# Expert down product in 512-column halves of two k-tiles, and the overflow branch at the second expert

## The chip, the cores and the metric

One core of a Trainium2 chip runs the kernel. The metric is the device time of one execution in microseconds (us); shown is the median of three runs. Engines: PE is TensorE (matmul), with PEld for its weight loads, DVE is VectorE, ACT is ScalarE, POOL is GpSimd, and SP is SyncE, whose queue issues the weight transfers from memory.

## What is computed

Two decoder layers on 256 tokens of 1024 features, all in float32. Layer 0 is a gated short convolution and a dense SwiGLU; layer 1 is dilated sliding-window attention and a mixture of experts. A final norm follows. The change touches the mixture alone:

```python
def moe_swiglu(h, w_router, w_gate, w_up, w_down):
    logits = jnp.einsum('bsd,de->bse', h, w_router)
    top_val, top_idx = lax.top_k(logits, TOP_K)            # 2 of 8
    top_w = jax.nn.softmax(top_val, axis=-1)
    gates = jnp.sum(jax.nn.one_hot(top_idx, N_EXPERTS) * top_w[..., None], axis=-2)
    for e in range(N_EXPERTS):
        out = out + gates[..., e:e + 1] * swiglu(h, w_gate[e], w_up[e], w_down[e])
```

`w_gate[e]` and `w_up[e]` are 1024 x 2816 and `w_down[e]` is 2816 x 1024, so each expert brings 34.6 MB of weights. The result is multiplied by the layer's gate row G (1024 values, the same for all tokens) and added to the residual x.

## The kernel before

The tokens of an expert are counted and placed in slots. A pair of experts gets its tokens gathered (`gather`, a product with a 0/1 matrix) as columns of `xg`, up to 128 per expert, in groups of 32. The first two groups are always computed. Groups 2 and 3 stand inside `by_groups`: a branch of PE on the count (over 64 at L1415, over 96 at L1417), which jumps over their instructions. More than 128 tokens of one expert go to `overflow()`, a long straight-line path behind a branch of PE, ACT, DVE and POOL at L1502, which stands ahead of expert 6 (`e == NE - 2`).

Per expert there are three rounds of gate and up products (1024, 1024 and 768 columns), each of two blocks of four loads, and then the down product in four blocks of 3, 3, 3 and 2 loads (`DOWN`). A load is two k-tiles, 1 MB in most. A block (`block`) takes its loads from the stream, multiplies them for groups 0 and 1, turns half of the activations of the round before (`turned`, `activated`), then branches to the other groups, then gives the loads back. `st.add_slot` lists the buffers for loads: at the end there are 17. SyncE issues the loads in the order of their use, each as soon as its slot is free.

A product keeps 32 token columns as weights and streams the expert's weight matrix through PE, four products side by side on four strips of 32 columns, so that a PSUM bank's 128 rows hold four results of 32 tokens. A float32 product shows in the trace as two LDWEIGHTS and two MATMUL. In gate/up (`use`, L1512 to L1517) the strips are gate and up times two halves of the columns, 512 columns each. In the down product (`use`, L1540 to L1544) they are four pieces of 256 of the 1024 output columns, and all k-tiles add up in the same rows. Four multiplications at L1554 weigh the four groups' banks with G4 (G in the same four pieces) into `og`.

PSUM: `groups()` gives four banks. Two are one of two `mm` tiles that are rotated each round (`sums_of`); the other two, for groups 2 and 3, are always the tile `rest`. The way back (`back`) runs after the first block of the next expert's first round: it multiplies `og` with a 0/1 matrix `GT` (`spread`) that puts each slot to its token, 32 rows at a time in four strips side by side, one piece of 256 columns each, into four banks (two halves of the other `mm` tile, two `tp` tiles), and eight DVE operations at L1493 add it to x with the token's weight.

The last expert runs its down product in three pieces of columns (`LAST`), with strips for k-tiles instead of columns, and has its own way back (`last_back`, L1561).

The order of instructions on each engine is that of the program; waits between engines come from the tiles that are written and read.

Of the kernel before, what the change touches and what calls it, by code (L numbers as in the profile page):

```python
# [10 lines left out]
F32 = mybir.dt.float32  # L11
# [7 lines left out]
P = 128  # L19
D = 1024  # L20
S = 256
# [31 lines left out]
def trunk_kernel(ctx: ExitStack, tc: tile.TileContext, a, out):  # L53
# [633 lines left out]
    slotc = cst.tile([P, 4], F32, name="slotc")  # L687
    slot = None

    def make_routing():  # L690
        nonlocal slot

        part = cst.tile([P, 4], I32, name="part")
        gp.iota(part, pattern=[[0, 4]], base=0, channel_multiplier=1)
        ve.tensor_scalar(part, part, 31, None, op0=OP.bitwise_and)
        partf = cst.tile([P, 4], F32, name="partf")
        ve.tensor_copy(partf, part)
        gp.iota(slotc, pattern=[[32, 4]], base=1, channel_multiplier=0, allow_small_or_imprecise_dtypes=True)
# [544 lines left out]
    def spread(e):  # L1243
# [5 lines left out]
        for g in range(4):  # L1249
            ve.tensor_scalar(GT[:, g], p[:, :S], slotc[:, g:g + 1], None, op0=OP.is_equal)  # L1250
# [110 lines left out]
    for n in range(2 * N_SPLIT):  # L1361
# [14 lines left out]
    st.add_slot("acc_g", lambda: [pers.tile([P, 1024], F32, name="rawa", tag="acc_g"),  # L1376
                                  moe.tile([P, 1024], F32, name="rawg")])
# [26 lines left out]
    G4 = moe.tile([P, 256], F32, name="G4")  # L1404
    for c in range(4):
        r = slice(32 * c, 32 * c + 32)
        sc.activation(G4[r], mods[3].G[r, 256 * c:256 * c + 256], AF.Copy)
# [67 lines left out]

    def back(e, n):

        ps = [sums_of[1][:, :512], sums_of[1][:, 512:], turn_tile(), turn_tile()]
        GT = GTs[e]

        def part(g):
            for i in range(NT):
                for c in range(4):
                    r = slice(32 * c, 32 * c + 32)
                    mm(ps[c][:, 256 * i:256 * i + 256], GT[r, g, i * P:(i + 1) * P], og[r, g], g == 0 and i == 0,
                       g == 3 and i == NT - 1)
        for g in range(2):
            part(g)
        by_groups(n, part)
        for i in range(NT):  # L1490
            for c in range(4):
                cs = slice(256 * c, 256 * c + 256)
                ve.scalar_tensor_tensor(x[:, i, cs], ps[c][:, 256 * i:256 * i + 256], gates[:, i, e:e + 1], x[:, i, cs],  # L1493
                                        op0=OP.mult, op1=OP.add)

    for e in range(NE):
        pr, b = divmod(e, 2)
        n_before, n_of = n_of, nc.values_load(counts[0:1, e:e + 1], engines=[mybir.EngineType.PE], min_val=0, max_val=S)
        if e == NE - 2:
# [53 lines left out]
        for g in range(4):  # L1553
            ve.tensor_mul(og[:, g], bank[g][:, :256], G4)  # L1554
# [90 lines left out]
```

## Time and profile before

| | |
|---|---|
| runs, median of three (lowest, highest) | 1230.16 us (1227.57, 1233.21) |
| the profiled execution, and its span | 1232.34 us, 1230.2 us |
| PE busy, PEld busy | 1103.3 us (90%), 671.8 us (55%) |
| DVE busy, ACT busy, POOL busy | 528.4 us (43%), 308.0 us (25%), 31.7 us (3%) |
[...]
| read from memory | 395.45 MB, 322 GB/s over the span |

An engine's busy time counts its instructions, not whether they ran at the engine's pace. Idle time before an instruction is put down to what ended last of what it waited for; "issue" is time in which it waited for nothing that the profile shows, and PEq is PE's own sequencer, as in a branch. A DMA share of 1 means that the core's 16 DMA engines were busy all the time (it can show a little more). Rows that the prediction uses stand in a section of their own below.

### The profile page before, as it was taken

The page shows a single profiled execution, that of the slowest core. Times are in us where ns is not written, and L with a number is a line of the kernel's source. Part 1 is how long each engine was busy: PE and PEld are TensorE (multiplying, and loading weights), DVE is VectorE, ACT ScalarE, POOL GpSimd, SP SyncE. Part 2 cuts the span into 40 slices and gives each one's busy share as a digit, 9 for nine tenths or more (in the row PEclk, how much of TensorE's full clock was granted, in tenths as well). Part 3 has the DMA queues.
Part 4 walks back from the last instruction along what each step waited for, and adds up shares of the span by engine and source line. Part 5 has one row for each costly group of instructions (what it writes and reads, how often), then busy time and mean ns, then how long its engine had stood idle before and what let it go on. Part 6 is the DMA issues. An engine that isn't in the chain of part 4 may idle for free. (4 is left out here: it accounts for less than half of the span.)

```text
span 1230.2 us, 23934 instructions
## 1 busy us (share of the span) xinstructions
PE 1103.3 (90%) x10346; PEld 671.8 (55%) x10346; DVE 528.4 (43%) x859; ACT 308.0 (25%) x497; POOL 31.7 (3%) x54
## 2 busy tenths in 40 slices
PE   3999979999999999987988998999999997697896
PEld 0799679998878876333343243435334434234333
DVE  1599768888779867320311210220211130130224
ACT  2344425444444473310110110110010020010021
POOL 3010100000001000000000000000000000000000
PEclk9899989999999999999989999999999998799999
DMA  6989767787837915999999999799689999799993
GB/s 248 331 313 342 241 244 269 278 320 291 307 113 279 338 55 196 406 407 407 404 408 405 404 408 395 274 395 399 225 344 405 361 388 407 288 365 407 405 373 125
DMA packets 139555, 398.82 MB, mean 324 GB/s; under 512 B 11427, under 2 KB 22459, under 8 KB 139402
## 3 DMA queue, kind: packets, MB, share of 16 engines
q1 hardware_dynamic: 138826, 396.47, 84.8%
q8 instruction: 125, 2.05, 0.7%
q14 instruction: 28, 0.23, 0.0%
q0 software_dynamic: 576, 0.07, 0.0%
HBM read 395.45 MB, written 1.05 MB: 322 GB/s over the span
## 5 line engine op out<-in xcount | busy, mean ns | idle before, releaser
L73 PE MATMUL mm<-raw,xg 128*32 128x512 f32 (+1 forms) x1624 | 234.7, 557 | 24.3 <-PEq L1502 8.1
L220 DVE TENSOR_TENSOR wlo<-raw,whi 128x1024 fp32r<-128x1024 f32 (+2 forms) x130 | 154.0, 1221 | 31.8 <-ACT whi L218 31.1
L218 ACT ACTIVATE whi<-raw 128x1024 fp32r<-128x1024 f32 (+2 forms) x130 | 132.2, 1045 | 126.3 <-PE mm L73 90.4
L1423 ACT ACTIVATE gu<-mm 64x512 f32<-64x512 f32 (+1 forms) x96 | 51.5, 551 | 447.5 <-PE mm L73 397.0
L73 PE MATMUL mm<-hTl,whi 128*128 128x256 f32 x544 | 148.6, 287 | 7.6 <-DVE hTl L531 7.6
L73 PE MATMUL mm<-rawr,xg 128*32 128x512 f32 (+1 forms) x1176 | 149.2, 570 | 5.8 <-PEq L1415 3.0
L73 PE MATMUL mm<-hTh,whi 128*128 128x256 f32 x544 | 151.3, 293 | 1.4 <-ACT hTh L530 1.4
L73 PE MATMUL mm<-hTh,wlo 128*128 128x256 f32 x544 | 147.9, 285 | 0.8 <-DVE wlo L220 0.8
L73 PEld LDWEIGHTS mm<-raw,xg 128*32 128x32 f32 x1624 | 70.5, 110 | 130.0 <-issue 120.8
L1424 DVE TENSOR_TENSOR gu<-gu,mm 64x512 f32<-64x512 f32 (+1 forms) x96 | 62.0, 646 | 182.0 <-ACT gu L1423 181.5
L73 PEld LDWEIGHTS mm<-hTl,whi 128*128 128x128 f32 x544 | 102.5, 194 | 10.9 <-DVE hTl L531 7.8
L73 PEld LDWEIGHTS mm<-hTh,whi 128*128 128x128 f32 x544 | 103.8, 198 | 3.9 <-ACT hTh L530 2.1
L73 PEld LDWEIGHTS mm<-hTh,wlo 128*128 128x128 f32 x544 | 102.4, 194 | 1.0 <-DVE wlo L220 1.0
L73 PE MATMUL mm<-rawr,acts 128*32 128x256 f32 x1280 | 80.3, 394 | 11.7 <-PEq L1415 3.9
L73 PE MATMUL mm<-raw,acts 128*32 128x256 f32 (+1 forms) x1168 | 79.0, 401 | 12.9 <-issue 5.6
L73 PEld LDWEIGHTS mm<-rawr,xg 128*32 128x32 f32 x1176 | 45.2, 110 | 79.1 <-issue 75.5
L1554 DVE TENSOR_TENSOR og<-mm,G 128x256 f32<-128x256 f32 x28 | 10.3, 418 | 178.2 <-PE mm L73 173.5
L73 PEld LDWEIGHTS mm<-rawr,acts 128*32 128x32 f32 x1280 | 42.9, 112 | 46.1 <-issue 18.7
L73 PEld LDWEIGHTS mm<-raw,acts 128*32 128x32 f32 x1168 | 41.2, 113 | 46.3 <-issue 25.1
L1435 DVE COPY acts<-tp 128x256 f32<-128x256 f32 (+1 forms) x48 | 19.3, 402 | 95.1 <-ACT acts L1241 94.7
L73 PE MATMUL mm<-rawx,xg 128*32 128x512 f32 (+1 forms) x272 | 56.0, 547 | 0.6 <-PEq L1417 0.5
L1493 DVE SCALAR_TENSOR_TENSOR x<-mm,gates,x 128x256 f32<-128x256 f32 x28 | 12.2, 477 | 97.6 <-PEq L1415 58.6
(271 smaller groups left out, 1462.6 us busy)
## 6 DMA issues: line engine op xcount, KB each, us to landing
rawr<-in_moe_w_down_dram SPq DMA_DIRECT2D x66, 512.0 KB, 10.1
raw<-in_mod_w_dram SPq DMA_DIRECT2D x64, 512.0 KB, 5.3
raw<-in_moe_w_down_dram SPq DMA_DIRECT2D x31, 1024.0 KB, 13.4
raw<-in_moe_w_gate_dram SPq DMA_DIRECT2D x26, 1024.0 KB, 12.2
raw<-in_moe_w_up_dram SPq DMA_DIRECT2D x25, 1024.0 KB, 12.8
rawr<-in_moe_w_up_dram SPq DMA_DIRECT2D x48, 512.0 KB, 11.5
rawr<-in_moe_w_gate_dram SPq DMA_DIRECT2D x48, 512.0 KB, 11.5
raw<-in_mod_w_dram SPq DMA_DIRECT2D x16, 1024.0 KB, 6.0
```

What stands on the lines that cost most here:

```text
L73: pe.matmul(o, l, r, start=start, stop=stop, skip_group_check=True)
L218: sc.activation(hi[:n, :c1 - c0], src, AF.Copy)
L220: ve.tensor_sub(lo_, src, f32(hi)))
L1423: sc.activation(a[64:, :N], bank[g][:64, :N], AF.Silu)
L1424: ve.tensor_mul(a[64 * g:64 * g + 64, :N], a[64:, :N], bank[g][64:, :N])
L1435: copy(acts[:, 8 * r:8 * r + 2 * nb, g:g + 32].rearrange("p (j m) t -> p m j t", j=2), v[:, :, n])
L1493: ve.scalar_tensor_tensor(x[:, i, cs], ps[c][:, 256 * i:256 * i + 256], gates[:, i, e:e + 1], x[:, i, cs], op0=OP.mult, op1=OP.add)
L1554: ve.tensor_mul(og[:, g], bank[g][:, :256], G4)
```

## The change

The down product takes two pieces of 512 columns instead of four of 256. The four strips are now two pieces times two k-tiles: strips 0 and 1 hold the sums of the even and the odd k-tile of each load for columns 0 to 511, strips 2 and 3 the same for 512 to 1023. `weighed` adds the halves: ACT copies the strip of one k-tile beside the other (32 x 512), DVE adds the two, and DVE multiplies with G2. Groups 0 and 1 are put one above the other, so that piece 0 of `og` has 64 rows per half of the columns; groups 2 and 3 are pieces 1 and 2 with 32 rows. The way back follows: piece 0 is one product of 64 rows and 512 columns for each tile of tokens and half, and DVE adds four results of 512 columns to x. The slot numbers that `spread` compares with get seven columns instead of four: three for this arrangement, four for the last expert's.

The place of G2 is that of `acc_g`, and the weight slot `acc_g` (with its other half `rawg`) is no longer given to the stream. The overflow branch stands ahead of expert 1 instead of expert 6.

```diff
--- before.py
+++ after.py
@@ -684,18 +684,21 @@
     upper = cst.tile([P, P], BF16, name="upper")
     ones_b = cst.tile([P, P], BF16, name="ones_b")
     ident_b = cst.tile([P, P], BF16, name="ident_b")
-    slotc = cst.tile([P, 4], F32, name="slotc")
+    slotc = cst.tile([P, 7], F32, name="slotc")
     slot = None
 
     def make_routing():
         nonlocal slot
 
-        part = cst.tile([P, 4], I32, name="part")
-        gp.iota(part, pattern=[[0, 4]], base=0, channel_multiplier=1)
-        ve.tensor_scalar(part, part, 31, None, op0=OP.bitwise_and)
-        partf = cst.tile([P, 4], F32, name="partf")
+
+        part = cst.tile([P, 7], I32, name="part")
+        gp.iota(part, pattern=[[0, 7]], base=0, channel_multiplier=1)
+        partf = cst.tile([P, 7], F32, name="partf")
+        for c, n, m, base, step in ((0, 2, 63, 1, 64), (2, 1, 63, 97, 0), (3, 4, 31, 1, 32)):
+            c = slice(c, c + n)
+            ve.tensor_scalar(part[:, c], part[:, c], m, None, op0=OP.bitwise_and)
+            gp.iota(slotc[:, c], pattern=[[step, n]], base=base, channel_multiplier=0, allow_small_or_imprecise_dtypes=True)
         ve.tensor_copy(partf, part)
-        gp.iota(slotc, pattern=[[32, 4]], base=1, channel_multiplier=0, allow_small_or_imprecise_dtypes=True)
         ve.tensor_add(slotc, slotc, partf)
         nc.sync.dma_start(rw, a["router_w"][0].rearrange("(k p) e -> p k e", p=P))
         gp.iota(tri, pattern=[[1, NE], [-1, NE]], base=0, channel_multiplier=0, allow_small_or_imprecise_dtypes=True)
@@ -1246,8 +1249,8 @@
         for i in range(NT):
             mm(p[:, i * P:(i + 1) * P], pxb[:, i], ident_b, i == 0, i == NT - 1)
         GT = moe.tile([P, 4, S], F32, name="GT")
-        for g in range(4):
-            ve.tensor_scalar(GT[:, g], p[:, :S], slotc[:, g:g + 1], None, op0=OP.is_equal)
+        for n, g in enumerate(range(3, 7) if e == NE - 1 else range(3)):
+            ve.tensor_scalar(GT[:, n], p[:, :S], slotc[:, g:g + 1], None, op0=OP.is_equal)
         GTs[e] = GT
 
     def overflow():
@@ -1373,8 +1376,6 @@
     remainder_h(1, 0)
     shifted(1, 1)
     st.add_slot("rows", lambda: pers.tile([P, 2048], F32, name="raw", tag="rows"))
-    st.add_slot("acc_g", lambda: [pers.tile([P, 1024], F32, name="rawa", tag="acc_g"),
-                                  moe.tile([P, 1024], F32, name="rawg")])
     st.topup()
     round_h(1, 1)
     most = moe.tile([P, 1], F32, name="most")
@@ -1401,10 +1402,10 @@
     ve.tensor_scalar(over, most, P + 0.5, None, op0=OP.is_gt)
     for t in turn_of:
         ve.memset(t, 0.0)
-    G4 = moe.tile([P, 256], F32, name="G4")
-    for c in range(4):
-        r = slice(32 * c, 32 * c + 32)
-        sc.activation(G4[r], mods[3].G[r, 256 * c:256 * c + 256], AF.Copy)
+    G2 = pers.tile([P, 512], F32, name="G2", tag="acc_g")
+    for h in range(2):
+        r = slice(64 * h, 64 * h + 64)
+        sc.activation(G2[r], mods[3].G[r, 512 * h:512 * h + 512], AF.Copy)
 
     fg = acts = og = n_of = pxb = None
     trans = None
@@ -1473,30 +1474,41 @@
         bk = [sums_of[0], rest]
         return [bk[g // 2][:, g % 2 * 512:g % 2 * 512 + 512] for g in range(4)]
 
+    def weighed(bank):
+
+
+        for g in range(4):
+            p, n = ((0, 0), (0, 1), (1, 0), (2, 0))[g]
+            for c in range(2):
+                r, q = (slice(k, k + 32) for k in (64 * c + 32 * n, 64 * c + 32 - 32 * n))
+                half = pers.tile([P, 512], F32, name="half", tag="rtmp", bufs=3)
+                sc.activation(half[r], bank[g][q], AF.Copy)
+                ve.tensor_add(og[r, p], bank[g][r], half[r])
+                if g != 0:
+                    r = slice(64 * c, 64 * c + (64 if g == 1 else 32))
+                    ve.tensor_mul(og[r, p], og[r, p], G2[r])
+
     def back(e, n):
 
-        ps = [sums_of[1][:, :512], sums_of[1][:, 512:], turn_tile(), turn_tile()]
+        ps = [[sums_of[1][:, :512], sums_of[1][:, 512:]], [turn_tile(), turn_tile()]]
         GT = GTs[e]
 
-        def part(g):
+        def part(p):
             for i in range(NT):
-                for c in range(4):
-                    r = slice(32 * c, 32 * c + 32)
-                    mm(ps[c][:, 256 * i:256 * i + 256], GT[r, g, i * P:(i + 1) * P], og[r, g], g == 0 and i == 0,
-                       g == 3 and i == NT - 1)
-        for g in range(2):
-            part(g)
-        by_groups(n, part)
+                for c in range(2):
+                    q = slice(64 * c, 64 * c + (32 if p else 64))
+                    mm(ps[i][c], GT[q, p, i * P:(i + 1) * P], og[q, p], p == 0, p == 2)
+        part(0)
+        by_groups(n, lambda g: part(g - 1))
         for i in range(NT):
-            for c in range(4):
-                cs = slice(256 * c, 256 * c + 256)
-                ve.scalar_tensor_tensor(x[:, i, cs], ps[c][:, 256 * i:256 * i + 256], gates[:, i, e:e + 1], x[:, i, cs],
-                                        op0=OP.mult, op1=OP.add)
+            for c in range(2):
+                cs = slice(512 * c, 512 * c + 512)
+                ve.scalar_tensor_tensor(x[:, i, cs], ps[i][c], gates[:, i, e:e + 1], x[:, i, cs], op0=OP.mult, op1=OP.add)
 
     for e in range(NE):
         pr, b = divmod(e, 2)
         n_before, n_of = n_of, nc.values_load(counts[0:1, e:e + 1], engines=[mybir.EngineType.PE], min_val=0, max_val=S)
-        if e == NE - 2:
+        if e == 1:
             engines = [mybir.EngineType.PE, mybir.EngineType.Activation, mybir.EngineType.DVE, mybir.EngineType.Pool]
             flag = nc.values_load(over[0:1, 0:1], engines=engines, min_val=0, max_val=1)
             with tc.If(flag > 0):
@@ -1538,10 +1550,10 @@
         bank = groups()
 
         def use(g, q, us):
-            for f in range(2):
-                for c in range(4):
-                    mm(bank[g][32 * c:32 * c + 32, :256], acts[:, 2 * q + f, 32 * g:32 * g + 32],
-                       us[0].at(f, 256 * c, 256), (q, f) == (0, 0), (q, f) == (FF // 256 - 1, 1))
+            for j in range(4):
+                c, f = divmod(j, 2)
+                mm(bank[g][32 * j:32 * j + 32], acts[:, 2 * q + f, 32 * g:32 * g + 32], us[0].at(f, 512 * c, 512),
+                   q == 0, q == FF // 256 - 1)
         for m, qs in enumerate(DOWN):
             block(n_of, [(1, q) for q in qs], use)
             if b == 1 and 0 < m < 3:
@@ -1549,9 +1561,8 @@
                     p = turn_tile()
                     gather(pr + 1, (2 * q, 2 * q + 1), (0, 1), p)
                     gathered(pr + 1, (2 * q, 2 * q + 1), p, act_copy)
-        og = moe.tile([P, 4, 256], F32, name="og")
-        for g in range(4):
-            ve.tensor_mul(og[:, g], bank[g][:, :256], G4)
+        og = moe.tile([P, 3, 512], F32, name="og")
+        weighed(bank)
 
 
     e = NE - 1
```

## Rows read from the trace of the kernel before

**Rows 1.** Windows: us, busy (count) by engine, clock, DMA share, GB/s

```profile
500.00:740.00 240.00, 214.60 (x2446) 92.75 (x2442) 47.76 (x106) 30.12 (x61) 0.00 (x0) 0.97 1.03 406
740.00:960.00 220.00, 204.54 (x2572) 91.69 (x2564) 34.58 (x74) 20.05 (x40) 0.00 (x0) 1.00 0.90 349
960.00:1000.00 40.00, 37.40 (x408) 14.33 (x400) 9.33 (x20) 3.88 (x8) 0.00 (x0) 1.00 0.94 356
1060.00:1100.00 40.00, 37.09 (x333) 12.81 (x337) 9.38 (x19) 5.44 (x11) 0.00 (x0) 0.93 0.76 284
1100.00:1200.00 100.00, 85.91 (x966) 35.85 (x958) 22.82 (x48) 13.06 (x28) 0.00 (x0) 0.98 1.03 396
```

**Rows 2.** What SyncE's queue waited for, 500 to 740 us: total us, times, longest

```profile
SPq L480 <- DMA rawr<-in_moe_w_down_dram: 31.2, 36, 1.0
```

**Rows 3.** What SyncE's queue waited for, 740 to 1100 us

```profile
SPq L480 <- PEq L1417: 137.3, 20, 12.0
```

**Rows 4.** Timeline of SyncE: first weight issue of expert 2 and of expert 6

```profile
633.10 0.38 SPq L480 DMA_DIRECT2D raw<-in_moe_w_gate_dram  x1
...
1007.91 0.66 SPq L480 DMA_DIRECT2D raw<-in_moe_w_gate_dram  x1
```

**Rows 5.** Timeline of PE, start of expert 6

```profile
1056.11 1.89 PE L73 MATMUL mm<-raw,xg 128*32 128x512 f32 x3 [8.14 <-PEq L1502]
1061.57 1.93 PE L73 MATMUL mm<-raw,xg 128*32 128x512 f32 x8 [3.57 <-issue]
```

**Rows 6.** Windows, down stages of experts 0, 1, 3, 4, 5

```profile
539.20:573.20 34.00, 24.75 (x355) 14.34 (x355) 2.94 (x6) 2.44 (x6) 0.00 (x0) 0.90 1.03 407
619.20:654.10 34.90, 28.63 (x387) 16.99 (x387) 3.87 (x11) 4.87 (x10) 0.00 (x0) 0.90 1.03 408
823.10:860.60 37.50, 35.40 (x572) 21.14 (x567) 3.81 (x10) 4.95 (x10) 0.00 (x0) 1.00 1.01 402
927.80:962.50 34.70, 31.55 (x542) 17.89 (x538) 2.96 (x7) 2.55 (x6) 0.00 (x0) 1.00 1.02 405
1010.60:1048.10 37.50, 29.14 (x387) 18.02 (x387) 3.87 (x11) 4.82 (x10) 0.71 (x1) 0.86 1.03 406
```

**Rows 7.** Windows, first gate/up rounds of experts 1, 6, 7

```profile
573.20:591.30 18.10, 16.16 (x160) 6.08 (x160) 4.69 (x12) 0.04 (x1) 0.00 (x0) 1.00 1.03 408
1048.10:1080.40 32.30, 20.16 (x160) 6.30 (x160) 4.59 (x12) 0.00 (x0) 1.29 (x1) 0.79 0.75 291
1140.50:1160.80 20.30, 16.16 (x160) 6.07 (x160) 4.74 (x12) 0.03 (x1) 0.00 (x0) 1.00 1.03 406
```

**Rows 8.** Line L1502, overflow branch: duration min/median/max ns, first and last start

```profile
L1502 PEldq COMPARE_BRANCH  x1: 6132/6132/6132, 1049.7 to 1049.7; - x1
...
L1502 DVEq EVENT_SEMAPHORE  x1: 21/21/21, 1054.6 to 1054.6; - x1
```

**Rows 9.** Timeline of PE: down matmuls, 256 columns, and 512 (last expert)

```profile
643.35 1.90 PE L73 MATMUL mm<-raw,acts 128*32 128x256 f32 x32
...
1188.42 1.92 PE L73 MATMUL mm<-rawr,acts 128*32 128x512 f32 x16 [0.18 <-DMA raw<-in_moe_w_down_dram]
```

**Rows 10.** Line L1415, branches over absent groups, as rows 8

```profile
L1415 PEldq COMPARE_BRANCH  x93: 70/223/6045, 501.5 to 1220.7; - x93
```

**Rows 11.** Timeline of PE in expert 5's down stage

```profile
1021.68 2.79 PE L73 MATMUL mm<-raw,acts 128*32 128x256 f32 x24 [4.73 <-PEq L1415]
```

**Rows 12.** Page, part 6, DMA issues: count, KB each, median us to landing

```profile
raw<-in_moe_w_down_dram SPq DMA_DIRECT2D x31, 1024.0 KB, 13.4
```

**Rows 13.** Groups by line and shape, 480 to 1230 us: busy us, mean ns

```profile
L1424 DVE TENSOR_TENSOR gu<-gu,mm 64x512 f32<-64x512 f32 x64 | 44.2, 691 | 138.5 <-ACT gu L1423 138.2
...
L1423 ACT ACTIVATE gu<-mm 64x512 f32<-64x512 f32 x64 | 36.6, 587 | 380.9 <-PE mm L73 344.8 <-DVE gu L1424 26.6 <-PEq L1417 9.6
```

**Rows 14.** Timeline of PE: the way back of expert 2, first and last matmuls

```profile
769.19 0.48 PE L73 MATMUL mm<-og,GT 32*128 32x256 f32 x2 [0.45 <-PEq L1417]
...
771.68 0.38 PE L73 MATMUL tp<-og,GT 32*128 32x256 f32 x2
```

## The prediction, made before the changed kernel was run

> **What bounds the kernel now.** I read the transfers first, because the second half of the program is mostly weights. By stretch [rows 1] they run at a DMA share of 1.03 and 406 GB/s from 500 to 740 us. That is as full as they get. From 740 to 960 us they fall to 349, and there are holes at 960 to 1000 (356) and at 1060 to 1100 us (284). So the expert part has two limits in turn. What SyncE's queue waited for tells which. From 500 to 740 us the longest entry is another DMA's landing, 31.2 us in 36 small pieces [rows 2]. From 740 to 1100 us it is PE's branch at L1417, 137.3 us in 20 waits [rows 3]: all weight slots are full and PE must free one. The issues show the lead. Expert 2's first weights were issued at 633.10 us and used after 654; expert 6's were issued at 1007.91 [rows 4] and used at 1056.11 [rows 5], 48 us later.
>
> Which expert is slow comes from its down stage: 540-odd matmuls in expert 4, 572 in expert 3, against 355 to 387 in experts 0, 1 and 5 [rows 6]. Experts 2, 3 and 4 run three token groups, the others two. So: experts 0 and 1 close to the pace of DMA, experts 2 to 4 at PE's pace with full slots, then DMA again from about 1085 us to the end, since after the hole at 1060 to 1100 us the transfers don't pause (share 1.03 again to 1200). A microsecond of hole after 960 us is therefore a microsecond at the end. PE's busy share over the whole span says little of this.
>
> **The hole at 1060 us.** Expert 6's first round takes 32.3 us, expert 7's (same count, 160 matmuls) 20.3 [rows 7]: 12.0 us more. PE waits 8.14 us for the branch at L1502, issues three matmuls, waits 3.57 us more with nothing to wait for, and the stage has a granted clock of 0.79 [rows 5, 7]. PE's compare-and-branch there lasts 6132 ns [rows 8]. It jumps over the whole overflow path. At 406 GB/s the stretch from 1060 to 1100 us lacks 40 x (1 - 284/406) = 12.0 us of transfers, the same 12.0.
>
> **The change, part by part.**
>
> *Overflow branch from expert 6 to expert 1.* It takes the 12.0 us out of expert 6, and the transfers then run on: **-12.0** at the end. It puts 12.0 into expert 1's first round, 18.1 now [rows 7].
>
> *Down product in 512 columns.* Per k-tile and group it streams 4 x 256 columns now, and 2 x 512 after. Streaming costs the same: 32 matmuls of 256 columns took 1.90 us, 16 of 512 columns 1.92 [rows 9]. What halves is the number of instructions, also of those that are jumped over where a group is absent: per piece of three loads 2 groups x 3 x 8 products before, 2 x 3 x 4 after. A gate/up block skips 2 x 16. The branches at L1415 take 223 ns in the median and up to 6045 [rows 10]. One of the long ones is in expert 5's down stage: PE restarts at 1021.68 after 4.73 us idle [rows 11]. The stages show what is lost: expert 4, three groups, 34.7 us at clock 1.00; expert 0, two groups, 34.0 us with 24.75 busy at 0.90 [rows 6]. A group's down product is 88 x 2 matmuls of 256 columns, 9.4 us at 8 in 0.43 us (what 1.90 us for 32 gives without the last one's tail). So without stalls expert 0 needs 34.7 - 9.4 = 25.3 (-8.7), and expert 1, which also gathers, 37.5 - 9.4 = 28.1 from expert 3 (-6.8). I take all of it: after the change a skipped piece (24 products) is smaller than a gate/up block's (32), and expert 7's first round, with such skips, runs at clock 1.00 [rows 7]. Bounds: nothing, and all of it.
> [...]
>
> *Expert 1's end.* PE: -8.7 + 12.0 - 6.8 = -3.5, so 650.6 for 654.1. DMA: its last weights are issued just before 633.10, land 13.4 us later in the median [rows 4, 12], about 645.5; with a slot less (below) 2.6 us later; the last piece (two loads, two groups, 3.4 us) ends at 651.5. The later counts: **-2.6**. Experts 2 to 4 carry it on at PE's pace.
>
> *One weight slot less* (acc_g): 1.05 MB at 406 GB/s, 2.6 us. While slots are full and PE sets the pace it is free. Where the pace goes over to DMA, after expert 4, DMA starts one load further back: **+2.6** (bounds 0 and 5.2, once more at the start).
>
> *Adding the halves.* New per expert: 8 ACT copies and 8 + 6 DVE operations of 512 columns, for four products. Nearest rows: 587 ns on ACT and 691 ns on DVE for 64x512 [rows 13]; fewer partitions I price alike. DVE: 14 x 0.69 = 9.7 us; ACT, 4.7 us, runs ahead. The way back reads the first piece after six DVE operations, about 5 us. It begins 8 us or more after the down product, behind half a round of gate/up (expert 0's product ended at 573, the next half round takes 6.9 us). The bank that groups 2 and 3 of the next expert write is read out last; that expert's group 2 comes about 10 us after, so 9.7 just fits. Zero; without that cover 2 to 5 us in each of experts 3 and 4.
>
> *Way back.* With three groups 24 products of 256 columns took from 769.19 to 772.06, 2.9 us [rows 14]. After: 8 products of 512 columns on 64 (or 32) rows. At 0.43 us a pass of 512 columns, two passes a product and two products side by side, 8/2 x 0.86 = 3.4. I take +0.6, three times, after experts 2 to 4: **+1.8**. Bounds: 0; and 8 x 0.86 = 6.9 if they run one by one, +12. With two groups it stays 1.7. The x updates lose instructions, off the path. Routing constants and G2 change by a few tiny operations: zero, in stages with idle ACT and POOL.
>
> *The end.* With DMA the limit through expert 7, PE meets late weights, and in stages where it did the clock was 0.90 [rows 6]: **+1.0** (bounds 0 and 3).
>
> Sum: -12.0 - 2.6 + 2.6 + 1.8 + 1.0 = **-9.2**. The profiled execution took 1232.34 us, 2.1 around its span; the median of three is 1230.16, 2.2 lower. From the median: **1221.0 us**.
>
> **Rivals.**
> 1. *The halves hold up the branch.* PE's first product after the branch writes a bank that the overflow path's DVE operations read, so it may wait until DVE has passed the branch too; DVE passes at 1054.6, PE's own branch ends at 1055.8 [rows 8]. Moved to expert 1, DVE first has 14 operations instead of 4, about 8 us more, and PE would start 6.7 us later. Uncovered, expert 1 ends at 657.3 (+3.2 in place of -2.6): -3.4, **1226.8 us**. For: DVE's and PE's times lie 1.2 us apart already. Against: PE's 3.57 us would pass meanwhile. Chance 0.2.
> 2. *Slower: the jumps cost what they did.* If the stall hangs on having jumped and not on the code's amount, experts 0 and 1 gain nothing, the moved branch puts the whole 12.0 ahead of PE's stretch, and expert 5 still fills the slots, so a hole as at 960 to 1000 us, 40 x (1 - 356/406) = 4.9, stays at expert 6: 12.0 - 7.1 + 1.8 + 2.6 = +9.3, **1239.5 us**. It decides from where about 10 of the 15.5 us of experts 0 and 1 stay. Against: long stalls in nearly every two-group down stage, few in gate/up, where less is skipped per time. Chance 0.13.
> 3. *The hole comes from the slots.* If expert 5 with 16 slots fills them anyway, the hole is not the branch's: -2.6 + 2.6 + 1.8 = +1.8, **1232.0 us**. Against: between experts 4 and 5, without the branch, it is only 4.9. Chance 0.1.
>
> Forecast 0.5; a remaining 0.07 for more, where the hole at 960 closes too: -14, 1216.
>
> **Numbers.** 0.5% is 6.2 us, about what a measurement of this kernel can tell from no change. Faster by more: forecast, its better case and a little of rival 1, 0.6. Same: most of rival 1, rival 3 and a forecast that falls short, 0.26. Slower: rival 2, and rival 1 together with a way back that runs one by one, 0.14. Range 1214 to 1234: from both holes closed to rival 3 with a second lost slot; rival 2 stays outside.
>
> **What would show it.** Right: no long branch at 1050 us, one of 5 to 6 us at about 565; transfers at 406 GB/s without a hole from 1000 us to the end; two-group down stages of 25 to 28 us at clock near 1.00; three-group stages unchanged; PE in expert 7 waiting for landings. Wrong: expert 0's and 1's down stages still near 34 us; expert 2 starting after 660 us; a hole at 1040 to 1090 us still; group 2 of experts 3 and 4 waiting for DVE.

## The result, and the profile after

The changed kernel took **1217.45 us** (median of 4 runs, 1214.77 to 1218.31) beside 1230.26 for the kernel before on the same chip: ratio 0.9892, 95% interval 0.9864 to 0.9919, 12.8 us less. Forecast were 1221.0 in a range of 1214 to 1234, and "faster by over 0.5%". Its profiled execution took 1217.71 us, with a span of 1215.9 and a mean granted clock of TensorE of 0.979 (0.972 before; the clock of every window is a share of TensorE's full speed).

The windows of rows 1, after the change:

```profile
500.00:740.00 240.00, 209.58 (x1906) 72.48 (x1902) 60.68 (x106) 37.90 (x75) 0.00 (x0) 0.95 1.03 406
740.00:960.00 220.00, 204.63 (x1880) 68.28 (x1876) 48.94 (x84) 29.45 (x56) 0.00 (x0) 1.00 0.88 338
960.00:1000.00 40.00, 37.41 (x328) 11.88 (x324) 16.90 (x26) 8.90 (x17) 0.00 (x0) 1.00 0.96 369
1060.00:1100.00 40.00, 37.63 (x318) 11.81 (x314) 8.54 (x17) 5.88 (x13) 0.00 (x0) 1.00 1.03 405
1100.00:1200.00 100.00, 86.81 (x716) 27.33 (x712) 31.97 (x55) 16.41 (x33) 0.00 (x0) 1.00 1.00 375
```

The hole at 1060 to 1100 us is closed: 405 GB/s for 284. The stretch from 740 to 960 us, where PE sets the pace, became slower in transfers, 338 for 349. The last row fell because the weights ran out: the last load landed at 1190.9 us (read from SyncE's issues and their landings), before at 1202.0.

What SyncE's queue waited for from 740 to 1100 us, then windows of the down stages of experts 0, 1, 4, 5 (from the first down matmul to the end of the last; [rows 6] has the ones before):

```profile
SPq L480 <- PEq L1418: 157.8, 23, 12.3
```

```profile
537.10:558.20 21.10, 20.35 (x179) 6.38 (x179) 2.94 (x6) 2.40 (x6) 0.00 (x0) 1.00 1.03 408
623.00:648.10 25.10, 24.37 (x211) 9.68 (x211) 3.82 (x10) 4.74 (x10) 0.00 (x0) 1.00 1.03 408
...
930.90:962.80 31.90, 30.55 (x270) 10.37 (x270) 2.51 (x5) 2.23 (x6) 0.00 (x0) 1.00 1.03 409
1010.40:1035.60 25.20, 24.43 (x211) 9.70 (x211) 3.81 (x10) 4.77 (x10) 0.71 (x1) 1.00 1.03 407
```

With two groups (experts 0, 1, 5) PE is busy for all but a microsecond, at clock 1.00: 21.1 us for 34.0, 25.1 for 34.9, 25.2 for 37.5. The slots are full as before while PE leads (157.8 us in 23 waits, [rows 3]).

The branches over absent groups (L1416 now, L1415 in [rows 10]), and the overflow branch (L1514, [rows 8]), each with duration min/median/max in ns and first and last start; last, PE's first product behind it, from the timeline:

```profile
L1416 PEldq COMPARE_BRANCH  x93: 70/208/1015, 499.3 to 1206.1; - x93
```

```profile
L1514 PEldq COMPARE_BRANCH  x1: 6073/6073/6073, 559.9 to 559.9; - x1
...
L1514 DVEq COMPARE_BRANCH  x1: 72/72/72, 570.2 to 570.2; - x1
...
L1514 DVEq EVENT_SEMAPHORE  x1: 21/21/21, 575.8 to 575.8; - x1
```

```profile
575.94 1.07 PE L73 MATMUL mm<-raw,xg 128*32 128x512 f32 x2 [17.70 <-DVEq L1514]
```

No branch at L1416 is long any more (1015 ns at most, for 6045). The overflow branch sits at 560 us, and PE's 6.07 us there are the smaller part: PE is through at 566.0 and waits for DVE until 575.9. DVE comes to its own branch at 570.2, behind the additions, and is through it only 5.6 us later. That is the mechanism of rival 1. (ACT's branch there takes 5.1 us, 568.7 to 573.8.)

The new operations in the page's groups, what PE waited for from 595 to 965 us, and the way back of expert 2 from the timeline ([rows 14]):

```profile
L1486 DVE TENSOR_TENSOR og<-mm,half 32x512 f32<-32x512 f32 x56 | 38.4, 685 | 157.6 <-ACT half L1485 156.5
...
L1485 ACT ACTIVATE half<-mm 32x512 f32<-32x512 f32 x56 | 32.9, 588 | 129.7 <-PE mm L73 90.3
```

```profile
PE mm L73 <- DVE og L1486: 6.1, 3, 3.3
```

```profile
766.31 1.13 PE L73 MATMUL mm<-og,GT 64*128 64x512 f32 x4 [0.45 <-PEq L1418]
...
769.19 1.02 PE L73 MATMUL tp<-og,GT 32*128 32x512 f32 x4
```

Prices per operation are as forecast (685 and 588 ns), but three times PE waits for DVE's og, each time in the first round of the next expert, ahead of its third token group: 3.28 us in expert 2, 1.43 each in experts 3 and 4. The first of them:

```profile
659.51 2.97 PE L73 MATMUL mm<-raw,xg 128*32 128x512 f32 x16 [3.28 <-DVE og L1486]
```

The way back takes 3.9 us (766.31 to 770.21) for 2.9.

To see where time went in each run I cut the span at three events: the first down matmul of expert 0, the end of expert 1's last down matmul, that of expert 4's, all read from the timelines of PE. The four parts of a row add up to its span.

| us, profiled execution | to expert 0's down | to the end of expert 1 | to the end of expert 4 | to the end | span |
|---|---|---|---|---|---|
| before | 539.3 | 114.7 | 310.1 | 266.1 | 1230.2 |
| **after** | 537.1 | 111.0 | 314.7 | 253.1 | 1215.9 |
| after, once more | 538.7 | 109.9 | 314.4 | 252.6 | 1215.6 |
| branch alone | 541.5 | 126.7 | 309.4 | 252.1 | 1229.7 |
| down alone | 540.4 | 107.9 | 312.5 | 257.5 | 1218.3 |
| code as before | 540.6 | 133.7 | 319.9 | 255.0 | 1249.2 |
| skipped code as before | 540.3 | 119.3 | 314.0 | 253.0 | 1226.6 |
| no overflow path | 538.6 | 107.9 | 312.5 | 252.9 | 1211.9 |
| one slot less | 538.3 | 109.7 | 314.0 | 255.8 | 1217.8 |
| order 2, 0, 3, 1 | 535.7 | 109.1 | 307.5 | 259.1 | 1211.4 |
| order 2, 0, 3, 1, POOL | 533.9 | 108.0 | 308.8 | 255.5 | 1206.2 |
| order 0, 2, 1, 3 | 540.5 | 109.0 | 307.5 | 253.4 | 1210.4 |
| order 0, 2, 1, 3, POOL | 531.8 | 108.4 | 307.8 | 252.9 | 1200.9 |

The first part is work that the change hardly touches; it differs by up to 6 us among kernels with the same operations there (the two POOL rows are another matter, in the last experiment). So the other three columns are the sharper measure; between the two executions of the changed kernel they differ by 1.1, 0.3 and 0.5 us. From before to after they give -3.7, +4.6 and -13.0 us. Forecast were -2.6, +1.8 and -8.4 (-12.0, +2.6 and +1.0).

### The profile page after: what moved, and what is told of

It reads as the page before. It is cut to its first block, busy times and chain, and to the rows that moved or that the text cites. A ratio compares the mean times of both kernels' runs of the same rounds, so it can differ in the third digit from the quotient of the medians.

```text
span 1215.9 us, 20659 instructions
## 1 busy us (share of the span) xinstructions
PE 1104.2 (91%) x8658; PEld 609.6 (50%) x8658; DVE 579.1 (48%) x896; ACT 340.6 (28%) x551; POOL 32.1 (3%) x56
## 3 DMA queue, kind: packets, MB, share of 16 engines
q8 instruction: 102, 1.67, 0.6%
## 5 line engine op out<-in xcount | busy, mean ns | idle before, releaser
L73 PE MATMUL mm<-raw,xg 128*32 128x512 f32 (+1 forms) x1616 | 241.1, 564 | 32.8 <-DVEq L1514 17.7
L73 PE MATMUL mm<-rawr,xg 128*32 128x512 f32 (+1 forms) x1360 | 168.1, 560 | 10.4 <-DVE og L1486 2.9
L1486 DVE TENSOR_TENSOR og<-mm,half 32x512 f32<-32x512 f32 x56 | 38.4, 685 | 157.6 <-ACT half L1485 156.5
L73 PEld LDWEIGHTS mm<-rawr,xg 128*32 128x32 f32 x1360 | 52.8, 110 | 100.0 <-issue 85.4
L73 PE MATMUL mm<-raw,acts 128*32 128x512 f32 (+1 forms) x784 | 86.5, 562 | 7.8 <-DMA raw<-in_moe_w_down_dram 4.8
L73 PE MATMUL mm<-rawr,acts 128*32 128x512 f32 x608 | 73.2, 595 | 3.0 <-PEq L1416 1.4
L1485 ACT ACTIVATE half<-mm 32x512 f32<-32x512 f32 x56 | 32.9, 588 | 129.7 <-PE mm L73 90.3
L73 PEld LDWEIGHTS mm<-raw,acts 128*32 128x32 f32 x784 | 25.0, 109 | 62.5 <-issue 50.5
L285 DVE SCALAR_TENSOR_TENSOR acc_ab<-raw,csil,acc_ab 128x1024 f32<-128x1024 f32 x40 | 51.3, 1282 | 6.6 <-DMA acc_ab<-in_mod_b_dram 5.9
L73 PE MATMUL mm<-whi,hTh 128*128 128x512 f32 (+1 forms) x128 | 49.8, 406 | 0.8 <-ACT hTh L530 0.7
## 6 DMA issues: line engine op xcount, KB each, us to landing
rawr<-in_moe_w_gate_dram SPq DMA_DIRECT2D x48, 512.0 KB, 11.2
```

The costliest lines, as they stand in the source:

```text
L73: pe.matmul(o, l, r, start=start, stop=stop, skip_group_check=True)
L285: ve.scalar_tensor_tensor(acc, w, csil[:, k:k + 1], acc, op0=OP.mult, op1=OP.add)
L1485: sc.activation(half[r], bank[g][q], AF.Copy)
L1486: ve.tensor_add(og[r, p], bank[g][r], half[r])
```

## The experiments

Ratios are to the kernel before on the same chip, with 95% intervals.

### 1. The branch alone, and the down product alone

To the kernel before:

```diff
-        if e == NE - 2:
+        if e == 1:
```

> The kernel before with the overflow branch alone moved to the second expert. Theory (the gain came from the down stages; the move of the branch gains nothing by itself): the two-group down stages of experts 0, 1 and 5 stay at 33 to 38 us, expert 1's first round goes from 18.1 to 28 to 31 us (DVE has only four operations ahead of its branch), expert 4 ends about 11 us later than before, and from there to the end it takes about 254 us for 266, since the hole of 12 us is gone: 1228 to 1233 us, no change. Rival (the move is what gained): expert 1's end is set by the landing of its weights, so the 12 us vanish there and the end comes 10 to 13 us earlier, 1217 to 1220 us.

Measured: 1226.87 us, ratio 0.998 (0.9963 to 0.9996). To the kernel after, the reverse:

```diff
-        if e == 1:
+        if e == NE - 2:
```

> The kernel after with the overflow branch alone put back to expert 6. Theory (the quick down stages leave the weight slots near empty at expert 6, so that the transfers run on while PE waits at the branch): the wait of 12 to 19 us stands at about 1040 us, the transfers from 1040 to 1100 us stay above 390 GB/s, and the time is that of the changed kernel within 3 us, 1215 to 1220 us. Rival (the forecast's first term: the branch's place at expert 6 cost 12 us): the hole in the transfers comes back and the time is 1227 to 1231 us.

Measured: 1220.13 us, ratio 0.9927 (0.9900 to 0.9954). Windows of the kernel with the branch alone (expert 0's down stage, and the stretch of the old hole):

```profile
541.50:576.90 35.40, 26.17 (x355) 15.03 (x355) 2.94 (x6) 2.41 (x6) 0.00 (x0) 0.86 1.03 407
```

```profile
1060.00:1100.00 40.00, 37.96 (x349) 14.09 (x352) 10.32 (x20) 5.65 (x11) 0.00 (x0) 0.96 1.03 403
```

and of the kernel with the down product alone, that stretch, and PE's wait ahead of it (waits of 1030 to 1060 us):

```profile
1060.00:1100.00 40.00, 38.51 (x366) 13.42 (x358) 12.39 (x22) 7.35 (x15) 0.00 (x0) 1.00 0.95 358
```

```profile
PE mm L73 <- DMA rawr<-in_moe_w_up_dram: 17.8, 1, 17.8
```

The branch alone closes the hole (403 GB/s) and pays for it at once: expert 1 ends 12.0 us later (126.7 for 114.7), and experts 2 to 4 carry that on. What is left, 2.2 us on the medians (1229.06 before on that chip), is at the edge of what can be told. So the rival, that expert 1's end hides the branch, falls here: its down stages still stall.

The down product alone brings 8.9 us, over two thirds of the gain, with the branch still at expert 6, where PE stands for 17.8 us. (The view names a weight load; PE's own branch there, 6.07 us from 1035.1, and DVE's at L1514 stand in the same stretch.) The hole is there but small: 40 x (1 - 358/406) = 4.7 us for 12.0. I had expected transfers above 390 GB/s, so the theory held in the time (1220.13 in 1215 to 1220 and a little) and not quite in the row. The reason is expert 5: its down stage takes 25.2 us for 37.5 (25.2 with the down product alone as well), so it gives slots back sooner, and they take up what comes in while PE stands. SyncE's timeline shows it, the last issue ahead of the hole and the first behind it, before and then with the down product alone:

```profile
1051.48 0.38 SPq L480 DMA_DIRECT2D raw<-in_moe_w_gate_dram  x1
1070.89 0.38 SPq L480 DMA_DIRECT2D raw<-in_moe_w_up_dram  x1
```

```profile
1050.07 0.38 SPq L480 DMA_DIRECT2D raw<-in_moe_w_up_dram  x1
1061.20 0.38 SPq L480 DMA_DIRECT2D raw<-in_moe_w_gate_dram  x1
```

Behind expert 5's last down product (1048.0 and 1033.5 us) the queue goes on for 3.9 us before, and for 16.9 us here, until all slots are full; then it stands for 19.0 and for 10.8 us.

### 2. How much code lies in a down stage

Token group 3 is absent for every expert, so its products are never executed. To the kernel after, only the code that is jumped over is changed:

```diff
-            for j in range(4):
+            for j in list(range(4)) * (5 if g == 3 else 1):
```

> The kernel after with the down products of token group 3 written five times in the body that is jumped over with these inputs (no expert has a fourth group), so that the code of a down stage has as many products as before while those executed stay halved. Theory (the stall is the fetching of code past the jumps, so it goes with the amount of code): the down stages of experts 0, 1 and 5 go back to 30 to 36 us and the time to 1228 to 1240 us. Rival (the number of executed instructions, or of jumps, sets it): these stages stay at 21 to 26 us and the time at 1215 to 1220 us.

Measured: 1249.97 us, ratio 1.0159 (1.0129 to 1.0189). With 3 in place of 5:

> The kernel after with the down products of group 3 written three times in the body that is jumped over. For an expert with two groups the code jumped over in a down stage is then what it was before (16 products for two k-tiles), with half as many products executed. Theory (what is skipped has to be fetched all the same, so the stall grows step by step with it): two-group down stages of 26 to 32 us, between the 21 to 25 of the changed kernel and the 33 to 36 measured with all the code of before; time 1223 to 1238 us. Rival (a threshold: the fetch keeps up as long as fewer products are executed): 21 to 26 us, 1215 to 1220 us.

Measured: 1228.53 us, ratio 0.9980 (0.9962 to 0.9997). Windows of expert 0's down stage and the branches at L1416, first with five times, then with three:

```profile
540.60:573.80 33.20, 23.76 (x179) 6.79 (x179) 2.94 (x6) 2.36 (x6) 0.00 (x0) 0.90 1.03 408
```

```profile
L1416 PEldq COMPARE_BRANCH  x93: 70/219/6157, 502.9 to 1239.5; - x93
```

```profile
540.30:569.00 28.70, 23.61 (x179) 6.69 (x179) 2.94 (x6) 2.32 (x6) 0.00 (x0) 0.94 1.03 407
```

```profile
L1416 PEldq COMPARE_BRANCH  x93: 70/218/6153, 502.5 to 1216.9; - x93
```

The same 179 matmuls take 21.1, 28.7 and 33.2 us as unexecuted code is added; before the change it was 34.0 with 355. The long branches come back, up to 6.2 us each. In 28.7 and 33.2 us PE is also busy for 3.3 and 3.4 us longer, as the mean granted clock falls from 1.00 to 0.94 and 0.90. Counted in products per piece of three loads, executed and jumped over: 24 and 24 after, 24 and 48 with three times, 24 and 72 with five, 48 and 48 before. So it isn't the jump alone: with the same 48 jumped over, 28.7 us stand against 34.0. What goes with the time is all the code of a piece, 48, 72 and 96 products for 21.1, 28.7 and 33.2 us, and 34.0 before with 96 too. The down stages of experts 0, 1 and 5 together say the same: 71.4, 86.3 and 104.4 us, before 106.4. Whether the executed half costs by its code or by its issue, no run takes apart.

The page's line for fetched code fits: 125 packets (2.05 MB) before, 102 (1.67 MB) after; then three times and five times:

```profile
q8 instruction: 102, 1.67, 0.6%
```

```profile
q8 instruction: 112, 1.84, 0.6%
```

```profile
q8 instruction: 122, 2.00, 0.6%
```

Ten packets more for each 616 products (seven experts, 11 loads, 8 products a load) that never run: the code that PE jumps over is fetched all the same.

Of expert 1 with three times the code the theory's range was met at its lower end only (26.1 us; expert 0 28.7, expert 5 31.5). With five times, experts 0, 1 and 5 take 33.2, 36.2 and 35.0 us, as expected or just above. The time lies 10 us above the range expected. 5.2 us of it stand in the third column (319.9 for 314.7), since the three-group experts now jump over 60 products a piece and stall too: a branch of 4168 ns at L1418 where 367 was the longest. 22.7 us stand in the second column, with the branch still at expert 1.

### 3. What the moved branch still costs

```diff
-        if e == 1:
+        if e == NE:
```

> The kernel after without the overflow branch and its path, which these inputs never take: the computation for experts with too many tokens is left out. It prices what the branch still costs at expert 1. Theory (expert 1's end is mostly set by the landing of its weights, and what is late there only partly reaches the end): expert 1's first round falls from 37 to 18 to 20 us, the end comes 0 to 5 us earlier, 1212 to 1217 us. Rival (the wait of PE for DVE at the branch is carried by PE's stretch in experts 2 to 4 to the end): 10 us or more earlier, 1203 to 1207 us.

Measured: 1215.09 us, ratio 0.9888 (0.9860 to 0.9915). That is 2.4 us below the changed kernel, but beside other runs of the kernel before; by the ratios (0.9888 for 0.9892) it is 0.5 us, well within the intervals. Windows of expert 1 up to its down product and of that product, without the branch:

```profile
559.70:616.50 56.80, 50.64 (x403) 14.93 (x404) 21.09 (x34) 10.85 (x21) 0.00 (x0) 1.00 1.03 406
616.50:646.50 30.00, 27.44 (x211) 10.03 (x211) 3.82 (x10) 4.75 (x10) 0.00 (x0) 1.00 1.03 408
```

PE's wait of 17.7 us is gone (the first round takes 20.7 us, where 18 to 20 were expected), but the gate/up rounds take 56.8 us where the same work took 48.2 in expert 6 (the down stage 30.0, for 25.1 after the change): PE now waits for landings, 6.4 us in expert 1 where the view names them. Of the 17.7 us, 3.1 reach the end of expert 1 (2.0 by the second execution of the changed kernel). The forecast's sentence that its end is set by the landing of its weights was right, and that is why rival 1's wait, larger than I had priced it, costs so little.

### 4. The weight slot

The slot `rows` is left out of the kernel after:

```diff
-    st.add_slot("rows", lambda: pers.tile([P, 2048], F32, name="raw", tag="rows"))
```

> The kernel after with one weight slot less (the one called rows). Theory (the forecast's term: with full slots up to expert 4 and transfers without a pause from there on, one load less ahead is one load later at the end): +2.6 us, 1219 to 1221 us. Rival (the slots are not what sets the time): within 1 us of the changed kernel.

Measured: 1220.48 us, ratio 0.9913 (0.9891 to 0.9935); 3.0 us above the changed kernel (by the ratios, which take the kernel before beside each, 2.6, or 1.4 against its second measurement in experiment 5), and 255.8 for 253.1 us in the last column. The intervals of the two kernels overlap, so the runs agree with 2.6 us a slot rather than prove it.

### 5. The order in which the halves are added

DVE and ACT alternate on a PSUM tile (groups 0 and 1 lie in one, 2 and 3 in the other): an ACT copy from a tile waits for the DVE addition before it on that tile, 0.75 us in the row below. ACT's second copy, and then the addition, in expert 0:

```profile
559.63 0.59 ACT L1485 ACTIVATE half<-mm 32x512 f32<-32x512 f32 x1 [0.75 <-DVE og L1486]
```

```profile
560.26 0.69 DVE L1486 TENSOR_TENSOR og<-mm,half 32x512 f32<-32x512 f32 x1 [0.66 <-ACT half L1485]
```

All four groups take 11.9 us (558.3 to 570.2, expert 0), and the tile that the next expert's groups 2 and 3 write is let go last. The order and the place of the multiplications change together here. To the kernel after:

```diff
-        for g in range(4):
+        for g in (2, 0, 3, 1):
...
-                if g != 0:
-                    r = slice(64 * c, 64 * c + (64 if g == 1 else 32))
-                    ve.tensor_mul(og[r, p], og[r, p], G2[r])
+        for p in range(3):
+            for c in range(2):
+                r = slice(64 * c, 64 * c + (32 if p else 64))
+                ve.tensor_mul(og[r, p], og[r, p], G2[r])
```

> The kernel after with the halves added in the order of groups 2, 0, 3, 1, all eight additions first and the six multiplications by G2 behind them. Theory (DVE's and ACT's hold on the bank that the next expert's groups 2 and 3 write is what makes PE wait for og in experts 2, 3 and 4, and PE sets the pace there): the three waits of PE for og vanish, expert 4 ends 5 to 8 us earlier, the time falls by 4 to 7 us to 1210 to 1214 us. Rival (the waits are covered by the landing of the weights later on): the waits vanish and the time stays within 1.5 us of the changed kernel.

Measured: 1216.47 us, ratio 0.9880 (0.9858 to 0.9902). The waits for the tile are gone and expert 4 ends 10.5 us earlier on the clock of its execution, 7.2 in the third column; then 6.0 of it are lost in the last one. Windows behind expert 4:

```profile
960.00:970.00 10.00, 7.94 (x28) 2.54 (x24) 5.16 (x8) 0.53 (x1) 0.00 (x0) 0.68 1.03 401
970.00:980.00 10.00, 9.66 (x72) 2.47 (x76) 2.72 (x5) 0.59 (x1) 0.00 (x0) 0.81 0.14 52
```

The way back of expert 4 waits 1.62 us for DVE, whose first piece is now complete only after all eight additions; the granted clock is 0.68 over these 10 us, after 1.00 until 960, and PE takes longer over its products there (2.08 us for the four of 32 rows that start at 965.72, where the changed kernel's expert 2 has 1.13 us for four); it frees slots late, and the transfers stop for most of 10 us (52 GB/s). The clock is not all of it: from 940 to 1010 us the transfers run at 386 GB/s in the changed kernel, at 350 in this order, and at 368 in the same order with the multiplications on POOL (below), where the clock stays at 1.00:

```profile
940.00:1010.00 70.00, 65.00 (x546) 22.36 (x542) 22.90 (x38) 12.72 (x25) 0.00 (x0) 0.93 0.90 350
```

```profile
940.00:1010.00 70.00, 65.14 (x573) 21.69 (x566) 20.81 (x38) 13.22 (x26) 7.54 (x6) 1.00 0.95 368
```

In 70 us these lack 6.2 and 3.1 us of transfers against 386, beside 6.0 and 2.4 us lost in the last column. Both the theory and the rival were half right. Two ways out, each with the multiplications still behind the additions: the order 0, 2, 1, 3, in which that piece is complete after six additions (`for g in (0, 2, 1, 3)`), and the multiplications on POOL (`gp.tensor_mul`).

> The order 0, 2, 1, 3 with the multiplications on DVE, all behind the additions: the order alone, without POOL. Theory (the clock's fall after expert 4 in the order 2, 0, 3, 1 on DVE came from the way back's wait for the first piece, which is 4 us longer on DVE than on POOL's side by side work): PE waits for DVE's og for 1 to 3 us in the way back, expert 4 ends near 950 us as in the other orders, and the time lies between 1203 and 1214 us, above that with POOL. Rival (POOL gives nothing, the order everything): within 1.5 us of the 1202.69 with POOL.

Measured, order 0, 2, 1, 3 on DVE: **1211.83 us**, ratio 0.9857 (0.9829 to 0.9885), and on the same chip

> The changed kernel once more, beside the next run, so that the two are set against each other on the same chip. Expected 1215 to 1219 us, as it first had (1217.45).

1217.28 us (ratio 0.9902, 0.9874 to 0.9930): 5.5 us less, and against the changed kernel's trace 7.2 us less in the third column with nothing lost behind it. Among the five largest waits of PE from 595 to 965 us none is for og any more, and the transfers of 740 to 960 us rise from 338 to 357 GB/s:

```profile
740.00:960.00 220.00, 206.25 (x1900) 67.92 (x1896) 51.66 (x88) 32.45 (x61) 0.00 (x0) 1.00 0.92 357
```

That 1 to 3 us of wait would remain in the way back was wrong (0.6 us is left); 1211.83 lies in the range. The shared tile is still the last to be read, but 8.8 us after the first copy (561.6 to 570.5) for 11.2 (558.3 to 569.5): neighbours in this order lie in different tiles, and the multiplications come later. Which of the two does how much isn't shown; the old order with the multiplications behind wasn't run.

> The same order, with the six multiplications by G2 moved from DVE to POOL. Theory: DVE reaches the overflow branch at expert 1 about 4 us sooner, PE's wait there falls from 17.7 to 11 to 14 us, of which 0 to 2 us reach the end beyond what the new order alone gives. Rival (POOL is slower with them, and the way back and the branch wait for POOL in DVE's place): PE's wait stays at 17 us or grows, the time is that of the new order alone or up to 3 us more.

Measured, order 2, 0, 3, 1 on POOL: 1208.07 us, ratio 0.9820 (0.9800 to 0.9840). PE's wait at the branch is 14.7 us, just above the 11 to 14 expected; the time is 8.4 us below the same order on DVE, where 0 to 2 were expected.

> As the run with the multiplications on POOL, but the groups added in the order 0, 2, 1, 3, so that the piece that the way back reads first is complete after six additions and not eight. Theory (what PE still waits for in the way back is POOL's og, 4.3 us in 7 waits, and it is set by when its first piece is complete): those waits fall to under 2 us, PE's wait at the end of an expert for the bank stays zero, the time falls by 0 to 3 us against the 1208.07 of the order 2, 0, 3, 1. Rival (the hold on the bank comes back, since its last reader is DVE's last addition either way and ACT reads it later): PE waits again for og of DVE in experts 2 to 4 and the time rises by 2 us or more.

Measured, order 0, 2, 1, 3 on POOL: **1202.69 us**, ratio 0.9770 (0.9745 to 0.9794), the best of all. The way back's wait for POOL falls from 4.3 us to 1.1, as expected, but the time by more than the 0 to 3 us. The table shows that POOL does little for the experts in this order (669.1 us behind the first column, 669.9 without POOL): PE's wait at the branch is 14.8 us for 16.1. What it gains lies in the first 10 us of the program. The first iota in POOL's timeline, without and with multiplications on it (order 0, 2, 1, 3), and the last two lines with them:

```profile
9.30 0.24 POOL L94 IOTA dif<- 128x128 f32 x1 [8.87 <-issue]
```

```profile
1.08 0.25 POOL L94 IOTA dif<- 128x128 f32 x1 [0.64 <-POOLq L1638]
...
1042.58 1.30 POOL L1520 PARTITION_BROADCAST fg<-fg  x1 [6.61 <-issue]
1101.87 7.99 POOL L1490 TENSOR_TENSOR og<-og,G 64x512 f32<-64x512 f32 x6 [57.98 <-DVE og L1486]
```

The first iota starts 8.2 us earlier, and expert 0's first down matmul 8.7 us (1.8 us in the order 2, 0, 3, 1). Over the twelve kernels with the late iota the first column averages 539 us, in the two with the early one 533. One more run asked what it takes, on the kernel after:

```diff
-                    ve.tensor_mul(og[r, p], og[r, p], G2[r])
+                    (gp if (e, g, c) == (0, 3, 1) else ve).tensor_mul(og[r, p], og[r, p], G2[r])
```

> The kernel after with one single multiplication out of the 42 on POOL, that of expert 0's group 3, whose product nobody reads with these inputs. It takes apart what the runs with POOL gained: in all eleven kernels without an arithmetic operation on POOL the program's first iota there began at 8.7 to 10.0 us, in the two with them at 1.1 us, and their expert parts are no quicker than the same order on DVE. Theory (that a POOL program holds one such operation is enough to let its first iota start early): iota at 1.1 us and 1217.4 - 8 = about 1209 us, 1206 to 1212. Rival (the early start belongs to the whole set of moved multiplications, or to chance): iota at 9 to 10 us, 1215 to 1219 us.

Measured: 1217.01 us, ratio 0.9907 (0.9883 to 0.9930), iota at 9.1 us. The theory falls: one multiplication early in the program does nothing. What all the traces have in common is the last operation on POOL: the broadcast in the twelve whose iota waits, the multiplications in the two whose iota does not. In the rows above, 6.61 us of "issue" stand ahead of the broadcast; ahead of the first iota it is 8.87 us in the kernel without multiplications on POOL, and 0.64 us of another wait with them. That the wait at the start hangs on the operation with which the execution before ended would fit all fourteen traces. It is the author's guess from these rows and not shown; a kernel whose last POOL operation is a small one behind the broadcast wasn't tried.

## Why the prediction was right

- **The overflow hole, -12.0.** Right in the sum: 284 to 405 GB/s is 40 x (405 - 284)/406 = 11.9 us. But the step laid the hole to the branch's place alone, and that failed. With the branch left at expert 6, the quicker down product shrinks it from 12.0 us to 4.7, and brings 8.9 of the 12.8 us; moved alone, the branch closes it and gives 2.2, as its 12 us then stand ahead of expert 1's end. The hole needed a stall at expert 6 *and* slots that are soon full there, and expert 5's quicker down stage puts the second off by 13 us. The forecast left expert 5's saving of 12 us out of the sum, as DMA sets the pace there; it is what closes most of the hole when the branch stays.
- **Two-group down stages, 25.3 and 28.1.** Direction and cause right, the size too small: 21.1 and 25.1. The step took three-group stages as free of stalls, and from windows that don't fit them: in [rows 6] expert 3's and 4's begin about 3 us early, in gate/up, and end 1.7 us early. From first to last down matmul they take 36.2 and 33.4 us (expert 2 33.9), and 35.9, 31.9 and 31.8 after the change, so "three-group stages unchanged" was wrong too, by 3.9 us in all. A group less is worth 10.8 us (31.9 - 21.1), not 9.4, since its branch of 0.45 us in each of three pieces goes too.
- **Rival 2, the jumps cost what they did.** With as many jumps and the same matmuls executed, group 3's code three times over (48 products of a piece jumped over for 24) takes expert 0's down stage from 21.1 to 28.7 us. The stall goes with the amount of code and not with having jumped alone: rival 2 falls.
- **Expert 1's end, -2.6.** -3.7 measured (-4.8 by the second execution), set by landings as said. Rival 1's mechanism came true at 9.9 us (566.0 to 575.9) for the 6.7 priced: DVE takes 11.9 us over the halves, not 9.7, mostly as it waits for the first copies, and then 5.6 us over its own branch. By the last three columns the whole branch at expert 1 costs 5.5 us (3.6 by the second execution), by the ratios 0.5, because the cover that rival 1 assumed gone was there.
- **Adding the halves, 0.** Wrong, and a sign of being wrong that the forecast itself named came true: group 2 of experts 3 and 4 waits for DVE. "9.7 just fits" was 2 us too optimistic. The price named for lost cover was 2 to 5 us in each of experts 3 and 4; measured are 3.28 us in expert 2, which was not priced, and 1.43 in each of the others. Another order with the multiplications behind gives 7.2 us back in experts 2 to 4: these 6.1 us and 1.1 of slow matmuls behind the first wait (2.97 us for 16, where 1.90 is usual, at a granted clock of 0.66 from 659 to 664 us).
- **Way back, +1.8.** +1.0 each (3.9 for 2.9), three times +3.0, with 0 to 12 as bounds. With 7.2 for the halves, and less 3.9 of down stages, the terms come to +6.3, where the third column has +4.6.
- **Slot, +2.6.** Agrees with the run without one more (+2.7 in the last column, +1.4 to 2.6 by the ratios).
- **The end, +1.0.** Wrong in sign: from the last weights' landing to the end it takes 25.0 us after (1190.9 to 1215.9) for 28.2 before. PE came out of the hole behind its weights, which I hadn't counted; the branch alone, which has no hole, takes 25.1 us (1204.6 to 1229.7). With the earlier hole (356 to 369 GB/s, 1.3 us) the last column adds up: -12.0 + 2.7 - 1.3 - 3.2 = -13.8, for -13.0 measured.
- **Rival 3** falls: with a slot less and no stall there is no hole.

The sum was 3.6 us short on the medians (-9.2 for -12.8), from terms that missed on both sides: the halves cost some 7 us, and the down stages and the end gave more than that. That it came so near is in part luck.

## What to carry to other kernels

Where PE jumps over absent work while weights stream (here at 406 GB/s), the code jumped over can cost as the executed code does (here 33.2 us for a stage with 24 products of a piece executed and 72 jumped over, 34.0 with 48 and 48): count the instructions of both, and write the bodies with fewer, wider ones. A stall of the engine that frees buffers hurts most where the buffers are soon full and nothing ahead of it runs late (here 12.0 us of transfers at expert 6, and 4.7 with a quicker stage ahead of it), so price a moved stall at its new place and ask whether something else removes it at the old one. Where PSUM is read in halves by two engines, let them alternate between tiles, put what doesn't read PSUM behind (5.5 us less here, both together), and look in the trace for the tile that the next stage writes and for the piece that the next reader takes: each should come early enough.

## What the runs showed of the hardware

- A jump past absent code stalled PE up to 6.2 us. A stage grew by 7.6 and 12.1 us (28.7 and 33.2 less 21.1) with 2 x 4 and 4 x 4 products a pair of k-tiles added in code that never ran, in which PE was busy for 3.3 and 3.4 us longer at a lower granted clock (0.94 and 0.90 for 1.00); the packets of fetched code rose from 102 to 112 and 122 (1.67, 1.84 and 2.00 MB).
- The branch over the overflow path took 6.07 us on PE, 5.6 on DVE and 5.1 on ACT in the changed kernel; PE, through at 566.0 us, waited for DVE, which came to it at 570.2, until 575.9.
- POOL's first iota starts at 1.1 us in the two kernels whose last operation on POOL is a multiplication, and at 8.7 to 10.0 in the twelve whose last one is the broadcast.
